# A feed-forward-heavy encoder block: another planning pass, another set of seven-product units, row factors moved to ScalarE

## The chip, the core and the metric

The kernel runs on one core of a Trainium2 chip. The metric is device time in microseconds for one execution; lower is better. The engines that matter are TensorE (PE, the matmuls), VectorE (DVE), ScalarE (ACT) and SyncE (SP), whose queue issues nearly all transfers. Each engine works through its own instructions in order, and they meet at semaphores.

## The reference

One layer of a streaming encoder with 256 rows of 2048 numbers in float32. It has four residual parts in a row and a last normalisation. The parts this case is about are the first and the last, two gated feed-forward nets with a hidden width of 5632:

```python
def swiglu(h, w_gate, w_up, w_down):
    return (jax.nn.silu(h @ w_gate) * (h @ w_up)) @ w_down

x = x + 0.5 * swiglu(rms_norm(x, ffn1_norm[l]), ffn1_w_gate[l], ffn1_w_up[l], ffn1_w_down[l])
h = rms_norm(x, mix_norm[l])
proj = h @ w_in[l]
...
x = x + jnp.concatenate([y_pool, y_gla], axis=-1) @ w_out[l]
x = x + mem_cross_attention(rms_norm(x, xattn_norm[l]), rms_norm(mem, mem_norm[l]),
                            xattn_w_q[l], xattn_w_kv[l], xattn_w_o[l])
x = x + 0.5 * swiglu(rms_norm(x, ffn2_norm[l]), ffn2_w_gate[l], ffn2_w_up[l], ffn2_w_down[l])
return rms_norm(x, final_norm)
```

`rms_norm` divides a row by its root mean square and multiplies by a gain. The row's divisor can be applied after a matmul, because it is one factor for the whole row; the kernel does that, and calls it the row factor, `Rcol`.

## The kernel before

**Numbers in two halves.** Every float32 operand is split into a high part, which ScalarE casts (`wh`, `xh`), and the rest, which VectorE subtracts (`wl`, `xl`). A product is then three matmuls: high by high, high by low, low by high (`products`, and the inner loop of `seven`).

**Units.** The work on weights is cut into units. A unit brings 1 MB of weights into a `raw` tile (128 partitions x 2048 numbers), splits it and multiplies it with the activations. There are four `raw` tiles and three `wh` and three `wl` tiles, so a split can be two units ahead of its matmuls. A `block_s` is eight units on one 1024-column block of the gate or up weights: 256 rows by 2 x 128 contraction rows by 1024 columns in each unit.

**Two kinds of unit.** A plain unit (`unit_p`) takes 8 products, so 24 matmuls of 512 columns. A unit of seven (`unit_s`, `seven`) uses a Strassen-Winograd scheme: 7 products, 21 matmuls. For it VectorE has to form four sums of quarter blocks in place, each reading or overwriting what the one before it used (`split_seven`: four additions `raw<-raw`), and two splits in place of one (`xh`, `xl` of 1536 numbers before the sums, `wh`, `wl` of 2048 after them). On the activation side the sums are formed once for a net (`part_sums`, `gate_sums`; they overwrite a part of `xs`, so a unit must have been used as a plain one before). `PAIRS` lists which of the eight units of a gate or up block are units of seven.

**PSUM.** There are four PSUM tiles, each of 2 x 512 numbers. A `block_s` needs all four: two for the products P1, P6, P7, P5 (`parts`), which `combine` empties as soon as the last unit of seven is done, and two (`ps`) in which P2, P3, P4 and all the plain products add up, and which are emptied at the block's end. A plain unit uses the second two only. The next block takes the tiles that were given back first. The transposes of the hidden values (`turn`) need two tiles for a while as well, and come a set number of units after their block.

**Evictions.** At a gate block's end VectorE adds `combine`'s sums to the products (`joined_to`, into a tile `sg`), and ScalarE applies `silu(Rcol * x)`. At an up block's end VectorE adds the sums in the same way and multiplies by the row factor and by the gate in two instructions (`ev_up`). Blocks come in the order gate, up, gate, up; an odd last block holds 512 columns of each (`wtwo`). The hidden columns are done in three parts of 4, 4 and 3 blocks of 512 (`FF_PARTS`), each followed by its down projection with its own pairs (`DOWN_PAIRS`), which the change doesn't touch.

**The planner.** The program first records every operation as a task with an engine, an estimated cost and what it depends on, then plans an order for each engine, and emits that order; the chip follows it. TensorE's matmuls keep the program's order except where one isn't ready. `latest` gives each task a latest start, backward from the end, without regard to what else its engine has to do. `schedule` then walks forward in time: an engine takes, of the tasks ready within 0.2 us (`WAIT`), the one with the smallest latest start. `ready` says when a task can begin: behind a task of another engine, at that task's end plus 0.034 us (`SYNC`) with its tail (0.085 us on VectorE); behind one of its own engine that only read what it overwrites, at once. All instructions appear in the profile under one line, L456, where the recorder issues them, so groups are told apart by their tiles.

Of the kernel before, what the change touches and what calls it, by code (L numbers as in the profile page):

```python
# [12 lines left out]
AF = mybir.ActivationFunctionType  # L13
ALU = mybir.AluOpType
# [190 lines left out]
class Plan:  # L205
# [104 lines left out]
    def ready(self, t, end):  # L310
        r = 0.0
        for p, data in t.preds.items():
            if p.engine is None:
                x = p.start
            elif p.engine == t.engine and not p.moved and (p.engine == "tensor" or not data):
                x = p.start + p.busy
            else:
                x = end[p.i] + self.SYNC
            r = max(r, x)
        return r  # L320

    def latest(self):
        for t in self.tasks:
            t.succs = []
        for t in self.tasks:
            for p in t.preds:
                p.succs.append(t)
        chain = [t for t in self.tasks if t.engine == "tensor"]
        behind = dict(zip(chain, chain[1:]))
        left = [len(t.preds) for t in self.tasks]  # L330
        for t in chain[1:]:
            left[t.i] += 1
        order = [t for t in self.tasks if not left[t.i]]
        for t in order:
            for s in (*t.succs, *([behind[t]] if t in behind else ())):
                left[s.i] -= 1
                if not left[s.i]:
                    order.append(s)
        assert len(order) == len(self.tasks)
        for t in reversed(order):  # L340
            late = -t.busy - t.tail
            for s in t.succs:
                if t.engine is None:
                    x = s.late
                elif t.moved:
                    x = s.late - 2.0 - t.moved / 338e3
                elif s.engine == t.engine and (t.engine == "tensor" or not s.preds[t]):
                    x = s.late - t.busy
                else:
                    x = s.late - t.busy - t.tail - self.SYNC  # L350
                late = min(late, x)
            if t in behind:
                late = min(late, behind[t].late - t.busy)
            t.late = late

    def schedule(self):
        self.share()
        self.latest()
        n = len(self.tasks)
        end, left = [0.0] * n, [len(t.preds) for t in self.tasks]  # L360
        free = {e: 0.0 for e in ("vector", "scalar", "tensor", "gpsimd", "sync")}
        waiting = {e: [] for e in free}
        tables, wire, out = {}, 0.0, []

        def release(t):
            todo = [t]
            while todo:
                t = todo.pop()
                for s in t.succs:
                    left[s.i] -= 1  # L370
                    if not left[s.i]:
                        s.start = self.ready(s, end)
                        if s.engine is None:
                            end[s.i] = s.start
                            out.append(s)
                            todo.append(s)
                        else:
                            waiting[s.engine].append(s)

        for t in self.tasks:  # L380
            if not t.preds:
                t.start = 0.0
                if t.engine is None:
                    out.append(t)
                    release(t)
                else:
                    waiting[t.engine].append(t)

        def pick(e):

            q, now = waiting[e], free[e]
            if e == "tensor":
                now = max(now, min(t.start for t in q))
                t = min((t for t in q if t.start <= now), key=lambda t: t.i)
                return now, t
            soon = max(now, min(t.start for t in q))
            u = min((t for t in q if t.start <= soon + self.WAIT), key=lambda t: t.late)
            if u.start > soon:
                fit = [t for t in q if t.start <= soon and soon + t.busy <= u.start]
                if fit:  # L400
                    u = min(fit, key=lambda t: t.late)
            return max(now, u.start), u

        while any(waiting.values()):
            at, t, _ = min(
                ((*pick(e), k) for k, e in enumerate(free) if waiting[e]),
                key=lambda x: (x[0], x[2]),
            )
            e = t.engine
            waiting[e].remove(t)  # L410
            t.start = at
            busy = t.busy * (2 if e == "tensor" and at < self.SLOW else 1)
            if t.table and tables.get(e) != t.table:
                tables[e] = t.table
                busy += 1.28
            free[e] = at + busy
            end[t.i] = at + busy + t.tail
            if t.moved:
                wire = max(wire, at + 2.0) + t.moved / 338e3
                end[t.i] = wire  # L420
            out.append(t)
            release(t)
        assert len(out) == n, (len(out), n)
        self.end = end
        out = [t for _, _, t in sorted((t.start, k, t) for k, t in enumerate(out))]
        return out

    WAIT = 0.2
    SLOW = 9.0

    def emit(self):
# [8 lines left out]
class Recorder:  # L440
# [3 lines left out]
    def __getattr__(self, name):  # L444
        def call(*args, **kw):
            plan, e = self.plan, self.engine
            views = [a for a in (*args, *kw.values()) if isinstance(a, View)]
            writes = [v for k, v in kw.items() if k in ("out", "accum_out") and isinstance(v, View)]
            if "out" not in kw and isinstance(args[0], View):
                writes.append(args[0])  # L450
            reads = [v for v in views if not any(v is w for w in writes)]

            def run():
                real = lambda a: a.resolve() if isinstance(a, View) else a
                f = getattr(getattr(plan.tc.nc, e), name)
                return f(*(real(a) for a in args), **{k: real(a) for k, a in kw.items()})  # L456

            t = plan.add(e, run, **cost(e, name, args, kw, writes, reads))
            t.f32 = e == "tensor" and name == "matmul" and args[1].dtype is F32
            t.what = (name, [v.buf.name for v in writes], [v.buf.name for v in reads])  # L460
            for v in reads:
                plan.touch(t, v, False)
            for v in writes:
                plan.touch(t, v, True)
            return t
        return call


def build(ctx, tc, I, out):
    nc = plan = Plan(tc)  # L470
    st = Stream()
# [69 lines left out]
    Rcol = ctl("Rcol", [P, 2])  # L541
# [3 lines left out]
    chain = ctl("chain", [P, 2, 8])  # L545
# [480 lines left out]

    FF_PARTS = ((0, 4), (4, 4), (8, 3))

    PAIRS = (0, 2, 4, 6)
    DOWN_PAIRS = {16: (2, 5), 12: (2, 4)}  # L1030
    OUT_PAIRS = (3, 5)

# [8 lines left out]
    def gate_sums(pairs):  # L1041

        for g in pairs:
            if not len(xe) % (len(PAIRS) + 1):
                xe.clear()
                xe["all"] = local([P, len(PAIRS), 2, 3, P], F32R, tag="xe", name=uid("xe"))
            xe[g] = xe["all"][:, PAIRS.index(g)]
            part_sums(xs, xe[g], g)

    def folded(c):  # L1050
        gate_sums([g for g in PAIRS[1:] if g // 2 == c])

    def ffn(wg, wu, wd, down, first=()):
        gate = {}
# [11 lines left out]
        def ev_gate(j, c, fresh):  # L1066

            if fresh and fresh == 1 + j:
                gate["new"] = hidden()
            g = gate["new"][j] if fresh else c  # L1070
            gate[j] = g
            for h in range(2):
                nc.scalar.activation(g[:, h, :], c[:, h, :], AF.Silu, scale=Rcol[:, h : h + 1])

        def ev_up(j, c):
            g = gate[j]
            for h in range(2):
                nc.vector.scalar_tensor_tensor(
                    out=g[:, h, :], in0=c[:, h, :], scalar=Rcol[:, h : h + 1], in1=g[:, h, :],
                    op0=ALU.mult, op1=ALU.mult,  # L1080
                )

        def turn(g, k):

# [8 lines left out]
        for lo, n in FF_PARTS:  # L1093
            for b in range(0, n - 1, 2):
                n0 = (lo + b) * NB
                pairs = first if lo == b == 0 else PAIRS
                if pairs:
# [306 lines left out]
    for b in range(2):  # L1404
        block_b(wblock(w_in, (4 + b) * NB), xs, ev_v(b))
        for i in range(2):
            h = 2 * b + i
# [229 lines left out]
            st.unit(wwide(wd, b * 2 * NB, k0 + nk - 2, 2)[0], end_unit(b))  # L1637
        st.op(second_half)

    st.op(lambda: gate_sums(PAIRS[:1]), 1)  # L1640
    ffn(I["ffn2_w_gate"][0], I["ffn2_w_up"][0], I["ffn2_w_down"][0], down_last, PAIRS[1:])
    st.op(close_scope)

# [64 lines left out]
```

## Time and profile before

| what | us |
|---|---|
| median of 3 runs | 2122.88 (2122.63 to 2125.29) |
| the profiled execution | 2122.68 |
| its span, first to last instruction | 2120.8 |
| granted TensorE clock, mean | 0.998 of full |
| HBM read and written | 417.58 MB and 16.78 MB |

The first net runs from the start to about 722 us, the mixer, attention and their projections to about 1397 us, the second net to the end. A profile's page lists busy time by engine, the span in 40 equal slices (a digit is the busy share in tenths), the chain of work that ended last, and the costliest groups of instructions. In a group's row stand the count, the busy time (overlaps counted once), the mean duration of one in ns, and the engine's idle time just before them with what ended it. A row of waits says which engine and tile waited for which, the total in us, how often, and the longest. A row of windows gives, for one stretch of time, its length and each engine's busy time with its number of instructions, then the granted clock, the DMA share and GB/s. A timeline row has start, duration, engine and instruction.

### The profile page before, as it was taken

The page shows a single profiled execution, that of the slowest core. Times are in us where ns is not written, and L with a number is a line of the kernel's source. Part 1 is how long each engine was busy: PE and PEld are TensorE (multiplying, and loading weights), DVE is VectorE, ACT ScalarE, POOL GpSimd, SP SyncE. Part 2 cuts the span into 40 slices and gives each one's busy share as a digit, 9 for nine tenths or more (in the row PEclk, how much of TensorE's full clock was granted, in tenths as well). Part 3 has the DMA queues.
Part 4 walks back from the last instruction along what each step waited for, and adds up shares of the span by engine and source line. Part 5 has one row for each costly group of instructions (what it writes and reads, how often), then busy time and mean ns, then how long its engine had stood idle before and what let it go on. Part 6 is the DMA issues. An engine that isn't in the chain of part 4 may idle for free.

```text
span 2120.8 us, 24464 instructions
## 1 busy us (share of the span) xinstructions
PE 2089.4 (99%) x9861; PEld 1732.5 (82%) x9861; DVE 1799.5 (85%) x1731; ACT 1102.5 (52%) x1002; POOL 15.8 (1%) x41
## 2 busy tenths in 40 slices
PE   9999999999999999999999999999999999999998
PEld 7878878788788888888888888887788877887886
DVE  7999889999899977688765545999998999988984
ACT  7555454554545645455654344556554455454543
POOL 0000000000000000000000000000000000000001
PEclk9999999999999999999999999999999999999999
DMA  7555756567565655457755555765567655675572
GB/s 280 197 195 203 257 199 212 188 234 245 182 220 207 240 181 181 157 179 258 239 182 174 164 174 159 238 199 199 179 218 258 214 186 184 229 254 202 185 273 98
DMA packets 143320, 435.94 MB, mean 206 GB/s; under 512 B 9828, under 2 KB 13000, under 8 KB 142824
## 3 DMA queue, kind: packets, MB, share of 16 engines
q1 hardware_dynamic: 143176, 434.38, 60.2%
q8 instruction: 77, 1.26, 0.2%
q14 instruction: 35, 0.29, 0.0%
q10 hardware_dynamic: 32, 0.01, 0.0%
HBM read 417.58 MB, written 16.78 MB: 205 GB/s over the span
## 4 chain that ended last, share of the span: by engine, by line
PE 54%; DVE 34%; issue 6%; ACT 3%; DMA 2%; SPq 0%; DVEq 0%; ACTq 0%
PE pt L456 27%; PE pa L456 15%; DVE wl L456 14%; DVE raw L456 8%; PE pb L456 6%; DVE xl L456 5%; DVE sg L456 5%; PE pe L456 3%; ACT wh L456 3%; DMA raw<-in_ffn_w_gate 1%; DVE ys L456 1%; DMA raw<-in_ffn_w_up 1%; DVE T L456 1%; DVE x L456 1%; PE pv L456 1%
## 5 line engine op out<-in xcount | busy, mean ns | idle before, releaser
L456 ACT CAST wh<-raw 128x2048 fp32r<-128x2048 f32 (+2 forms) x383 | 718.4, 1885 | 630.8 <-DVE raw L456 323.5
L456 DVE TENSOR_TENSOR wl<-raw,wh 128x2048 fp32r<-128x2048 f32 (+2 forms) x382 | 856.7, 2258 | 198.6 <-ACT wh L456 197.6
L456 PE MATMUL pt<-wh,xs 128*128 128x512 f32 x1820 | 590.4, 391 | 6.5 <-DVE sg L456 4.5
L456 PE MATMUL pt<-wh,ys 128*128 128x512 f32 x1392 | 441.3, 390 | 0.0
L456 PEld LDWEIGHTS pt<-wh,xs 128*128 128x128 f32 x1820 | 342.8, 188 | 78.3 <-issue 6.4
L456 PE MATMUL pt<-wl,xs 128*128 128x512 f32 x910 | 359.6, 395 | 7.4 <-DVE wl L456 7.2
L456 PE MATMUL pa<-xs,wh 128*128 128x512 f32 x912 | 320.1, 397 | 0.0
L456 DVE TENSOR_TENSOR raw<-raw 128x512 f32<-128x512 f32 x444 | 306.8, 691 | 13.4
L456 PEld LDWEIGHTS pt<-wh,ys 128*128 128x128 f32 x1392 | 261.2, 188 | 54.7 <-issue 0.2
L456 PE MATMUL pt<-wl,ys 128*128 128x512 f32 x696 | 271.2, 390 | 0.5 <-DVE wl L456 0.5
L456 PE MATMUL pa<-xs,wl 128*128 128x256 f32 x896 | 248.5, 280 | 0.0
L456 ACT CAST xh<-raw 128x1536 fp32r<-128x1536 f32 x111 | 164.5, 1482 | 153.6 <-PE pt L456 45.0
L456 PEld LDWEIGHTS pt<-wl,xs 128*128 128x128 f32 x910 | 171.4, 188 | 54.3 <-DVE wl L456 20.6
L456 PEld LDWEIGHTS pa<-xs,wh 128*128 128x128 f32 x912 | 170.8, 188 | 39.8 <-issue 0.7
L456 DVE TENSOR_TENSOR xl<-raw,xh 128x1536 fp32r<-128x1536 f32 x111 | 194.3, 1750 | 9.3 <-ACT xh L456 9.1
L456 PEld LDWEIGHTS pa<-xs,wl 128*128 128x128 f32 x896 | 169.1, 189 | 1.2
L456 PEld LDWEIGHTS pt<-wl,ys 128*128 128x128 f32 x696 | 130.7, 188 | 28.4 <-DVE wl L456 1.9
L456 DVE TENSOR_TENSOR sg<-pt,sg 128x1024 f32<-128x1024 f32 (+1 forms) x147 | 140.8, 966 | 9.9 <-ACT sg L456 7.0
L456 PE MATMUL pb<-wh,xs 128*128 128x512 f32 x384 | 121.9, 392 | 0.0
L456 PE MATMUL pt<-wh,xe 128*128 128x512 f32 x332 | 121.1, 393 | 0.0
L456 PE MATMUL pt<-xh,xs 128*128 128x512 f32 x332 | 119.6, 390 | 0.6 <-DVE sg L456 0.6
L456 PEld LDWEIGHTS pb<-wh,xs 128*128 128x128 f32 x384 | 72.1, 188 | 15.2 <-issue 0.3
(179 smaller groups left out, 1777.4 us busy)
## 6 DMA issues: line engine op xcount, KB each, us to landing
raw<-in_ffn_w_down SPq DMA_DIRECT2D x88, 1024.0 KB, 5.5
raw<-in_ffn_w_up SPq DMA_DIRECT2D x80, 1024.0 KB, 5.1
raw<-in_ffn_w_gate SPq DMA_DIRECT2D x77, 1024.0 KB, 5.1
raw<-in_w_in SPq DMA_DIRECT2D x32, 1024.0 KB, 5.2
raw<-in_xattn_w_kv SPq DMA_DIRECT2D x32, 1024.0 KB, 5.3
raw<-in_w_out SPq DMA_DIRECT2D x16, 1024.0 KB, 5.6
raw<-in_xattn_w_q SPq DMA_DIRECT2D x16, 1024.0 KB, 5.2
raw<-in_xattn_w_o SPq DMA_DIRECT2D x16, 1024.0 KB, 5.4
```

The costliest lines, as they stand in the source:

```text
L456: return f(*(real(a) for a in args), **{k: real(a) for k, a in kw.items()})
```

## The change

1. In the planner, an engine's own earlier tasks are no longer free to follow: any dependence, except between two TensorE tasks, costs the tail and `SYNC`.
2. VectorE's costs are taken 1% higher (`MARGIN`).
3. `schedule` alternates up to six forward walks (`forward`, the walk of before) with backward ones (`backward`), which place tasks from the end with one engine doing one thing at a time and so set new latest starts. The forward walk with the earliest end, by the model, is kept.
4. `PAIRS` becomes (1, 2, 4, 5). What is written in terms of `PAIRS` moves with it: the transposes of a pair of blocks come after six units of the next block and not seven, the second net's first sums after two units and not one.
5. The row factor of the up product goes into the gate: ScalarE multiplies the gate by `Rcol` once more after the silu, and `ev_up` is one product of 1024 columns.

```diff
-            elif p.engine == t.engine and not p.moved and (p.engine == "tensor" or not data):
+            elif p.engine == t.engine == "tensor":
                 x = p.start + p.busy
...
-                elif s.engine == t.engine and (t.engine == "tensor" or not s.preds[t]):
+                elif s.engine == t.engine == "tensor":
                     x = s.late - t.busy
...
     def schedule(self):
         self.share()
         self.latest()
+        best = None
+        for _ in range(self.ROUNDS):
+            out, end = self.forward()
+            if best is None or max(end) < best[0]:
+                best = max(end), out, end, [t.start for t in self.tasks]
+            self.backward()
+        _, out, self.end, starts = best
+        for t, at in zip(self.tasks, starts):
+            t.start = at
+        return out
+
+    ROUNDS = 6
+
+    def backward(self):
...
+        by = {t.i: t.start for t in self.tasks}
+
+        def bound(t):
+
+            x = 0.0
+            for s in t.succs:
+                if t.engine is None:
+                    x = min(x, s.late)
+                elif t.moved:
+                    x = min(x, s.late - self.SYNC - 2.0 - t.moved / 338e3 + t.busy)
+                elif s.engine == t.engine == "tensor":
+                    x = min(x, s.late)
+                else:
+                    x = min(x, s.late - t.tail - (self.SYNC if s.engine else 0.0))
+            return x
...
+        def pick(e):
+            q, now = waiting[e], free[e]
+            if e == "tensor":
+                for x, t in q:
+                    if t is chain[-1]:
+                        return min(now, x), (x, t)
+                return None
+            soon = min(now, max(x for x, _ in q))
+            x, t = max((c for c in q if c[0] >= soon - self.WAIT), key=lambda c: by[c[1].i])
+            return min(now, x), (x, t)
+
+        while any(waiting.values()):
...
+            t.late = at - t.busy
+            free[e] = t.late
+            release(t)
...
+    def forward(self):
...
     WAIT = 0.2
+    MARGIN = 1.01
...
             t = plan.add(e, run, **cost(e, name, args, kw, writes, reads))
+            if e == "vector":
+                t.busy *= plan.MARGIN
...
-    PAIRS = (0, 2, 4, 6)
+    PAIRS = (1, 2, 4, 5)
...
             for h in range(2):
                 nc.scalar.activation(g[:, h, :], c[:, h, :], AF.Silu, scale=Rcol[:, h : h + 1])
+            for h in range(2):
+                nc.scalar.activation(g[:, h, :], g[:, h, :], AF.Copy, scale=Rcol[:, h : h + 1])
 
         def ev_up(j, c):
-            g = gate[j]
-            for h in range(2):
-                nc.vector.scalar_tensor_tensor(
-                    out=g[:, h, :], in0=c[:, h, :], scalar=Rcol[:, h : h + 1], in1=g[:, h, :],
-                    op0=ALU.mult, op1=ALU.mult,
-                )
+            nc.vector.tensor_tensor(out=gate[j], in0=c, in1=gate[j], op=ALU.mult)
...
-    st.op(lambda: gate_sums(PAIRS[:1]), 1)
+    st.op(lambda: gate_sums(PAIRS[:1]), PAIRS[0] + 1)
     ffn(I["ffn2_w_gate"][0], I["ffn2_w_up"][0], I["ffn2_w_down"][0], down_last, PAIRS[1:])
```

More of the change, by code (lines that the diff above doesn't have):

```diff
@@ L358, in schedule, with release @@
         self.latest()
+        best = None
[10 more added lines that the diff above has]
+    def backward(self):
+        n = len(self.tasks)
+        for t in self.tasks:
+            t.late = None
+        left = [len(t.succs) for t in self.tasks]
+        free = {e: 0.0 for e in ("vector", "scalar", "tensor", "gpsimd", "sync")}
+        waiting = {e: [] for e in free}
+        wire = [0.0]
+        by = {t.i: t.start for t in self.tasks}
[11 more added lines that the diff above has]
+            return x
+        def release(t):
+            todo = [t]
+            while todo:
+                t = todo.pop()
+                for p in t.preds:
+                    left[p.i] -= 1
+                    if not left[p.i]:
+                        if p.engine is None:
+                            p.late = bound(p)
+                            todo.append(p)
+                        else:
+                            waiting[p.engine].append((bound(p), p))
+        for t in self.tasks:
+            if not t.succs:
+                if t.engine is None:
+                    t.late = 0.0
+                    release(t)
+                else:
+                    waiting[t.engine].append((-t.tail, t))
+        left_on = {e: sum(t.engine == e for t in self.tasks) for e in free}
+        chain = [t for t in self.tasks if t.engine == "tensor"]
+        def pick(e):
[9 more added lines that the diff above has]
+        while any(waiting.values()):
+            e, at, c = None, None, None
+            for k in free:
+                if waiting[k]:
+                    got = pick(k)
+                    if got and (at is None or got[0] > at):
+                        e, (at, c) = k, got
+            t = c[1]
+            waiting[e].remove(c)
+            if e == "tensor":
+                chain.pop()
+            t.late = at - t.busy
+            free[e] = t.late
+            release(t)
+        for t in self.tasks:
+            assert t.late is not None
@@ L423, in schedule @@
         assert len(out) == n, (len(out), n)
-        self.end = end
         out = [t for _, _, t in sorted((t.start, k, t) for k, t in enumerate(out))]
-        return out
+        return out, end
     WAIT = 0.2
+    MARGIN = 1.01
     SLOW = 9.0
```

## The prediction

> **What bounds the kernel now.** I read the page first, for who is busy where.
>
> ```profile
> span 2120.8 us, 24464 instructions
> PE 2089.4 (99%) x9861; PEld 1732.5 (82%) x9861; DVE 1799.5 (85%) x1731; ACT 1102.5 (52%) x1002; POOL 15.8 (1%) x41
> ...
> DVE  7999889999899977688765545999998999988984
> ...
> PE 54%; DVE 34%; issue 6%; ACT 3%; DMA 2%; SPq 0%; DVEq 0%; ACTq 0%
> ```
>
> TensorE is busy all the time, yet a third of the chain that ended last is VectorE. VectorE's nines lie in slices 2 to 14 and 27 to 38: the two feed-forward nets. So two engines run nearly level there. The windows cut by stage say how much TensorE loses. The gate and up stages are rows 1, 3, 4, 5 and 6; row 2 is a down projection.
>
> ```profile
> core 0: us, PE busy (x) PEld busy (x) DVE busy (x) ACT busy (x) POOL busy (x), PEclk, DMA share, GB/s
> 269.79:439.40 169.61, 167.54 (x738) 135.91 (x736) 162.41 (x140) 90.89 (x63) 0.00 (x0) 1.00 0.58 204
> 439.40:525.99 86.59, 86.53 (x389) 71.38 (x388) 80.27 (x70) 41.03 (x27) 0.00 (x0) 1.00 0.67 231
> 525.99:653.72 127.73, 125.73 (x558) 102.31 (x556) 120.43 (x100) 66.67 (x44) 0.00 (x0) 1.00 0.60 208
> 1397.28:1572.60 175.32, 170.93 (x757) 137.89 (x756) 171.56 (x174) 103.56 (x91) 0.00 (x0) 1.00 0.58 197
> 1659.39:1829.01 169.62, 167.51 (x737) 135.93 (x736) 162.32 (x140) 89.45 (x62) 0.00 (x0) 1.00 0.59 203
> 1915.61:2044.75 129.14, 126.91 (x558) 103.67 (x556) 120.56 (x100) 65.05 (x43) 0.00 (x0) 0.99 0.60 206
> ...
> 454.66 64.04 PE pt L456 x282
> ...
> 660.62 1.03 PE L456 MATMUL ph<-ident,sg 128*128 128x128 f32 x8
> ```
>
> The last two rows give TensorE's pace where nothing stops it: 64.04 / 282 = 0.227 us for a matmul of 512 columns, and about 0.11 us for a 128-column transpose (eight in 1.03 us, with the last one's tail). A unit of seven products has 21 such matmuls, 4.77 us; a plain one 24, 5.45 us. Row 1 is four blocks of four units each, 4 x (84 + 96) = 720 matmuls, 163.5 us, and 16 transposes, 1.7 us: 4.4 us of 169.6 are lost. In the same way the others lose 3.4 (540 matmuls), 7.6 (723, and 32 transposes), 4.4 and 4.8 us, and the down stage 0.4. That is **24.6 us in five stages**, the most that they can give back. VectorE is 93 to 98% busy in them.
>
> Who ends the waits, and what VectorE's steps cost:
>
> ```profile
> PE pt L456 <- DVE wl L456: 8.6, 19, 1.5
> PE pt L456 <- DVE sg L456: 5.0, 5, 1.1
> ...
> PE pt L456 <- ACT xs L456: 2.0, 1, 2.0
> ...
> 403.27 1.75 DVE L456 TENSOR_TENSOR xl<-raw,xh 128x1536 fp32r<-128x1536 f32 x1
> 405.05 2.87 DVE L456 TENSOR_TENSOR raw<-raw 128x512 f32<-128x512 f32 x4
> 407.84 4.49 DVE L456 TENSOR_TENSOR wl<-raw,wh 128x2048 fp32r<-128x2048 f32 x2
> 412.24 1.75 DVE L456 TENSOR_TENSOR xl<-raw,xh 128x1536 fp32r<-128x1536 f32 x1
> ```
>
> From 403.27 to 412.24 VectorE does one unit of seven and one plain: 8.97 us. The two wl take 4.40 to the next start, 2.20 each, so a plain unit costs VectorE **2.2 us** and one of seven **6.8 us**, against 5.45 and 4.77 us of TensorE. A block's units take 36 us of 41; sums, evictions and transposed splits bring VectorE level with TensorE or past it. Three buffers of split weights let it be two units ahead of TensorE, no more.
>
> **The change, part by part.** *Row factors on ScalarE.*
>
> ```profile
> L456 DVE TENSOR_TENSOR sg<-pt,sg 128x1024 f32<-128x1024 f32 x77 | 92.7, 1220 | 2.1
> L456 DVE SCALAR_TENSOR_TENSOR sg<-sg,Rcol,sg 128x512 f32<-128x512 f32 x40 | 27.8, 745 | 0.1
> L456 ACT ACTIVATE sg<-sg,Rcol 128x512 f32<-128x512 f32 x40 | 25.9, 713 | 18.1 <-DVE sg L456 18.1
> L456 ACT COPY sg<-pt 128x512 f32<-128x512 f32 x35 | 20.5, 586 | 85.9 <-PE pt L456 80.2 <-DVE wl L456 5.7
> ...
> 654.97 1.34 ACT L456 ACTIVATE sg<-sg,Rcol 128x512 f32<-128x512 f32 x2
> 657.66 1.40 DVE L456 SCALAR_TENSOR_TENSOR sg<-sg,Rcol 128x512 f32<-128x512 f32 x2
> ```
>
> ev_up drops two scalar_tensor_tensor and adds one 1024-wide product. By busy time, which counts overlapped tails once, that is 2 x 27.8/40 = 1.39 against 92.7/77 = 1.20 us: 0.19 us saved; by mean durations, 2 x 745 - 1220 = 270 ns. The nearest row of the product reads PSUM and the new one reads SBUF alone; I take no gain for that. There are 11 column blocks in each net, so 22 x 0.19 = **4.1 us** less VectorE work (5.9 by durations). Some falls where VectorE has room, so I count 3.3.
> ScalarE gets 44 scaled copies of 0.59 to 0.71 us, 26 to 31 us. It is 52% busy, and in a full pair of blocks the scaled gate is read a whole block later, some 40 us, so the copies hide behind its idle time. Without that cover they stand before the wh casts, 1.2 to 1.4 us a block. The tight place is the odd block at a part's end, where gate and up share one block: silu at 654.97, product at 657.66 to 659.06, transposes at 660.62. Two copies more take up most of the 1.6 us left there; I price it at 0, at worst 1.2 us twice.
>
> *PAIRS.* Two things move. First, the sums' evacuation (combine) now comes after the sixth unit, with two plain units behind it, and the next block starts plain. What it does today at a boundary, in the chain of waits and TensorE's timeline:
>
> ```profile
> 305.63 1.92 ACT wh L456
> ...
> 307.57 2.29 DVE wl L456
> 309.87 0.61 DVE sg L456
> ...
> 310.50 1.24 DVE sg L456
> ...
> 311.76 0.70 DVE sg L456
> ...
> 312.60 0.47 PE L456 MATMUL pt<-wh,xs 128*128 128x512 f32 x1 [1.12 <-DVE sg L456]
> ...
> 1957.50:1959.20 1.70, 0.62 (x3) 0.18 (x2) 1.56 (x3) 0.33 (x1) 0.00 (x0) 1.00 0.85 188
> 1959.20:1962.50 3.30, 3.27 (x8) 2.63 (x9) 3.30 (x3) 2.00 (x4) 0.00 (x0) 0.53 0.54 221
> ```
>
> VectorE waited for the wh cast, did a 2.29 us wl, and only then combine, while the next block's first products wanted the same PSUM tiles. Today they have one plain unit, 5.45 us, to come free; after the change two, 10.9 us, and the new block first takes the tiles that were freed earliest. So the five sg waits, 5.0 us, should go. With each goes about 0.2 us of restart (the 1.12 us wait stands for a start-to-start of 1.51 us instead of 0.23). At 1957 two of them lie together and the granted clock falls to 0.53 for 3.3 us: another 1.6 us. In all some 7.5 us.
> The Trainium skill (TensorE: Matmul & The Clock Gate, "Why this matters for your kernels") lets the clock fall only behind idle gaps of about 3 us. By that rule the 1.6 us isn't the gap's and stays. The trace disagrees: the fall follows waits of 0.6 and 1.1 us.
> The ACT xs wait, 2.0 us, is the second net's late S3 part, made for the new block's first unit of seven; that unit now comes second, 5.45 us later. It should go too. Sum of waits that lose their cause: 7.5 + 2.2 = 9.7 us.
> But VectorE works on without a pause behind these places, so part of what TensorE gains there it meets again as a wl wait. I take half, **4.9 us** (ends 0 and 9.7).
> Second, two units of seven now stand side by side twice a block. That is a demand, priced as a rival below.
>
> *The planner.* It counts 0.119 us for every dependent VectorE step; before, a step that only overwrites what the last one read was free. The rows above decide who is right.
>
> ```profile
> L456 DVE TENSOR_TENSOR raw<-raw 128x512 f32<-128x512 f32 x444 | 306.8, 691 | 13.4
> ```
>
> Four raw steps in a row take 2.87 us where 4 x 0.691 = 2.76: each starts 0.03 us after its predecessor's end. Independent wl overlap: 4.49 for two of 2.29, 0.09 before the end. So a dependent step costs 0.12 us more, as the new plan says; the old one left out three per unit of seven, 444/4 = 111 units x 0.36 = 40 us of VectorE work, and took the engine for freer than it is.
> The Trainium skill (VectorE: DVE Perf Modes, "Rules for kernel authors") says of chained steps that the drain "happens regardless" and only the number of operations counts. By that rule the new term would be an error and the order would get no better. The trace disagrees, by the 0.12 us.
> A truer plan makes no work vanish; it can move what isn't due out of the way of wl. Up to six forward and backward passes are tried and the best end in the model is kept. Of the 8.6 us of wl waits I count 1.5 (ends -3 and 8.6).
>
> **Sum.** 3.3 + 4.9 + 1.5 = 9.7 us. The profiled execution took 2122.68 us, its span 2120.8; the median of the three runs is 2122.88, so both stand for one state. 2122.7 - 9.7 = **2113 us**.
>
> **Rivals.** One more window belongs here, from the boundary shown above to the last late wl of the stage:
>
> ```profile
> 309.87:454.22 144.35, 142.28 (x634) 115.08 (x633) 142.26 (x125) 79.94 (x57) 0.00 (x0) 1.00 0.57 197
> ```
>
> *VectorE's work is the bound (2120).* In this window VectorE is busy for 142.26 of 144.35 us, so only its work counts there, and a wait removed comes back as another. Against it: row 1 has 169.61 - 162.41 = 7.2 us of VectorE idle, 5 us of it ahead of 309.87, which a smoother order could use. It would leave 3.3 us or less: 2119.4 to 2123. That the plan's order comes out almost as before ends here too.
> *The plan recovers most (2102).* If order and buffers are the fault and not work, 20 of the 24.6 us come back; the idle 7.2 us of row 1, more than its 4.4 us of loss, allow it. 2098 to 2106.
> *Side by side (2130).* From a block's first unit to its second pair, VectorE owes evictions of 4 x 1.2 = 4.8 us, four units of seven (27.2) and one plain (2.2): 34.2 us, against 2 x 5.45 + 3 x 4.77 = 25.2 us of TensorE. It must be 9.0 us ahead. Today's worst stretch, from the end of the seventh unit to the third of the next block, is combine 2.5 (the three sg rows above), evictions 2.4 + 2.8, units 6.8 + 2.2 + 6.8: 23.5 us against 15.7, so 7.8 us ahead. If the lead that the buffers allow lies between, each boundary of the ten pairs loses up to 1.2 us, and no gain of the waits remains: 2122.7 - 3.3 + 12 = 2131, or 2127 if two thirds of it come. It decides when wl waits come in front of a block's sixth unit. Against it: two units, about 10 us, is more than 9.0.
>
> **How the numbers follow.** Forecast 0.50 (2107 to 2118), plan recovers most 0.23, work bound 0.18, side by side 0.09. About 0.2% (4.2 us) is what a measurement of this kernel can tell from no change, so faster ends at 2118.6 and slower begins at 2127.1. Faster: 0.50 + 0.23 + 0.03 of the work bound's edge = 0.76; same 0.16; slower 0.08, with 0.01 of the side-by-side case inside no change. The range, 2100 to 2122, leaves out the lower edge of the recovery case (0.05), the upper one of the work bound (0.03) and the side-by-side case (0.09).
>
> **What would show it.** Right: no sg wait before a pt matmul and no clock of 0.53 at a boundary; raw, wl and xl groups as before in number; the SCALAR_TENSOR_TENSOR group on sg gone, 22 products of about 1.2 us in its place and 44 ScalarE copies near 0.6 us; the five stages together 6 to 12 us shorter. Wrong: wl waits that grow by what the sg waits lose (work bound), or that stand before the sixth unit of a block (side by side); transposes of the odd block waiting for sg (the copies' price); a loss in the mixer or the attention between 722 and 1397 us, which I expect unchanged within 2 us.

## The result and the profile after

The changed kernel takes 2107.48 us (median of 4 runs, 2106.91 to 2110.4) against 2122.76 before (four runs beside them): ratio 0.9929, 95% interval 0.9912 to 0.9947, 15.3 us less. Forecast were 2113 us and a range of 2100 to 2122. The profiled execution is the longest of the four, 2110.4 us with a span of 2108.6, so the profile shows 12.2 of the 15.3 us.

The page after, the lines that answer to those of before:

```profile
span 2108.6 us, 24534 instructions
PE 2083.8 (99%) x9861; PEld 1734.4 (82%) x9861; DVE 1790.3 (85%) x1709; ACT 1133.0 (54%) x1046; POOL 15.8 (1%) x41
...
PE 64%; DVE 21%; ACT 6%; issue 5%; DMA 4%; SPq 0%; ACTq 0%; DVEq 0%
```

TensorE's work is the same (x9861), and its share of the chain that ended last rose from 54 to 64%: VectorE holds it up less. The same five stages, cut anew at their own borders (columns as before):

```profile
266.49:435.40 168.91, 167.28 (x738) 135.97 (x736) 165.29 (x136) 96.01 (x69) 0.00 (x0) 1.00 0.59 210
...
521.52:647.53 126.01, 125.29 (x557) 102.66 (x556) 122.37 (x100) 69.78 (x49) 0.00 (x0) 1.00 0.59 213
1389.18:1566.22 177.04, 171.63 (x756) 139.44 (x755) 170.49 (x168) 109.07 (x97) 0.00 (x0) 0.99 0.57 195
1652.34:1820.03 167.69, 166.80 (x738) 136.16 (x736) 163.79 (x135) 95.53 (x69) 0.00 (x0) 1.00 0.59 206
1906.12:2032.36 126.24, 125.64 (x557) 102.43 (x556) 123.27 (x100) 68.35 (x47) 0.00 (x0) 1.00 0.61 217
```

Together 765.9 us against 771.4: 5.5 us of the 12.2. Four are shorter; the second net's first stage, is 1.7 us longer. Most of the rest lies where the forecast didn't look, shown here before and then after for the first net's first stage, its last down projection, and the mixer and attention:

```profile
6.58:183.33 176.75, 174.03 (x775) 142.36 (x774) 164.45 (x176) 108.63 (x119) 0.00 (x0) 1.00 0.64 225
653.72:722.26 68.54, 67.10 (x303) 53.84 (x302) 65.82 (x71) 36.58 (x41) 0.00 (x0) 1.00 0.62 222
722.26:1397.28 675.02, 675.02 (x3593) 578.53 (x3592) 471.82 (x519) 340.92 (x388) 5.28 (x12) 1.00 0.59 193
```

```profile
6.83:180.38 173.55, 173.17 (x776) 142.09 (x774) 163.23 (x169) 112.97 (x125) 0.00 (x0) 1.00 0.65 229
647.53:714.24 66.71, 66.02 (x302) 54.12 (x300) 63.53 (x68) 37.60 (x42) 0.00 (x0) 1.00 0.62 218
714.24:1389.18 674.94, 674.94 (x3594) 578.96 (x3592) 472.82 (x520) 341.56 (x388) 5.26 (x12) 1.00 0.59 193
```

3.2 and 1.8 us shorter, and the middle of the kernel unchanged. The other three down projections are 0.5 to 0.7 us shorter each. TensorE's waits after:

```profile
PE pt L548 <- DVE wl L548: 7.6, 14, 1.4
...
PE pt L548 <- ACT xs L548: 0.8, 1, 0.8
PE pt L548 <- DVE x L548: 0.6, 2, 0.3
```

The five sg waits (5.0 us) are gone, and the wl waits went down with them, 8.6 to 7.6 us. That was not a matter of course: the forecast let half of what is gained at the boundary come back there.

### The profile page after: what moved, and what is told of

The parts are those of the page before. It is cut to its first block, busy times and chain, and to the rows that moved or that the text cites. A ratio compares the mean times of both kernels' runs of the same rounds, so it can differ in the third digit from the quotient of the medians.

```text
span 2108.6 us, 24534 instructions
## 1 busy us (share of the span) xinstructions
PE 2083.8 (99%) x9861; PEld 1734.4 (82%) x9861; DVE 1790.3 (85%) x1709; ACT 1133.0 (54%) x1046; POOL 15.8 (1%) x41
## 4 chain that ended last, share of the span: by engine, by line
PE 64%; DVE 21%; ACT 6%; issue 5%; DMA 4%; SPq 0%; ACTq 0%; DVEq 0%
PE pt L548 37%; PE pa L548 15%; DVE wl L548 8%; PE pb L548 6%; DVE raw L548 5%; DVE xl L548 3%; ACT wh L548 3%; PE pe L548 3%; DMA raw<-in_ffn_w_gate 2%; DVE sg L548 2%; DMA raw<-in_ffn_w_up 2%; ACT sg L548 2%; DVE x L548 1%; PE ph L548 1%; PE pv L548 1%
## 5 line engine op out<-in xcount | busy, mean ns | idle before, releaser
L548 DVE TENSOR_TENSOR raw<-raw 128x512 f32<-128x512 f32 x444 | 306.7, 691 | 12.2
L548 PEld LDWEIGHTS pb<-wh,xs 128*128 128x128 f32 x384 | 72.1, 188 | 15.2 <-issue 0.2
```

## The experiments

Three theories stood against each other. **Boundary:** the gain comes from where evictions fall around a block's end. **Work:** VectorE's work is the bound, and 4 us less of it is what counts. **Plan:** the order was at fault. Each part was tried alone and each was taken out. The table gives medians and ratios against the runs of before that were made beside them (2122.2 to 2123.0 us).

| kernel | planner | PAIRS | row factor on | us | ratio, 95% interval |
|---|---|---|---|---|---|
| planner only | new | old | VectorE | 2118.76 | 0.9982 (0.9973 to 0.9990) |
| PAIRS only | old | new | VectorE | 2118.14 | 0.9978 (0.9969 to 0.9987) |
| rows only | old | old | ScalarE | 2125.97 | 1.0019 (1.0010 to 1.0028) |
| without rows | new | new | VectorE | 2107.05 | 0.9928 (0.9916 to 0.9941) |
| without PAIRS | new | old | ScalarE | 2114.31 | 0.9955 (0.9942 to 0.9967) |
| without planner | old | new | ScalarE | 2118.05 | 0.9980 (0.9971 to 0.9989) |

**Planner only.** The changed kernel with the old PAIRS and the old `ev_up`.

```diff
-    PAIRS = (1, 2, 4, 5)
+    PAIRS = (0, 2, 4, 6)
...
```

> Before with the planner's part alone (dependent steps counted, 1% margin, six passes); PAIRS (0, 2, 4, 6) and the row factor on VectorE as before. Boundary theory (the gain is the place of the evictions): 2120 to 2122 us, the sg waits before pt still about 5 us. Work theory (VectorE's work is the bound): no change, 2122 to 2123. Plan theory (the order was at fault): 2112 or less, the sg waits gone though PAIRS are the old ones.

3.4 us by medians, inside no theory's range. No sg wait before pt is left, though the PAIRS are the old ones; TensorE's waits name wl 11.1 us instead. So the order alone can take those waits away, and they come back elsewhere. They come back in long pieces, and the granted clock (the third number from the end of a window row) falls with them, by TensorE's waits, its timeline and the windows:

```profile
PE pt L548 <- DVE wl L548: 11.1, 14, 2.4
...
PE pt L548 <- ACT xs L548: 3.1, 1, 3.1
...
1779.62 0.50 PE L548 MATMUL pt<-wl,xs 128*128 128x512 f32 x1 [2.44 <-DVE wl L548]
...
387.77:391.18 3.41, 2.92 (x7) 2.23 (x8) 3.41 (x4) 2.28 (x2) 0.00 (x0) 0.50 0.55 137
1439.08:1442.49 3.41, 3.41 (x10) 2.73 (x10) 3.41 (x3) 0.00 (x0) 0.00 (x0) 0.50 0.54 217
1521.00:1527.83 6.83, 5.81 (x18) 4.84 (x19) 5.52 (x5) 3.42 (x3) 0.00 (x0) 0.50 0.55 166
1780.41:1783.82 3.41, 3.41 (x13) 2.92 (x12) 3.41 (x3) 1.18 (x2) 0.00 (x0) 0.50 0.89 294
```

Three of the four stretches come with a wl wait of 2.4 us right behind the transposes of `turn`, seven units into the next block; the other comes with the wait for ACT xs. The clock is at half for 17.1 us, and TensorE is busy for 15.6 of them, work that takes half as long at the full clock: an estimate of some 8 us lost, where the kernel before loses 1.6 in its one such stretch. The profiled execution is not a chance one: all eleven show a mean clock of 0.994 to 0.996, and the twenty-seven of before that were made beside them 0.998 on average. So, by this estimate, most of what the planner could give alone goes into these stretches.

**PAIRS only.** The edit above the other way round, in the kernel before, with the second net's first sums after `PAIRS[0] + 1` units.

> Before with PAIRS (1, 2, 4, 5) alone, old plan, row factor on VectorE. Boundary theory: 2112 to 2116 us, no sg wait before pt. Work theory: 2121 to 2123, wl waits grow by what the sg waits lose. Plan theory: with the old plan the side-by-side units cost, 2122 to 2128.

4.1 us, between the ranges of boundary and work. TensorE's waits of this kernel:

```profile
PE pt L456 <- DVE wl L456: 11.5, 27, 1.0
...
PE pt L456 <- DVE sg L456: 1.0, 1, 1.0
```

Four of the five sg waits went (5.0 to 1.0 us), and wl waits rose from 8.6 to 11.5: most of it came back, as the work theory has it. The 2.0 us wait for ACT xs and the stretch of 0.53 clock are gone too.

**Rows only.** `ev_gate` and `ev_up` as in the change, all else before.

> Before with the row factor on ScalarE alone. Work theory: 4.1 us of VectorE work less, 2118 to 2119 us. Boundary theory: the waits have another cause than work, 2120 to 2122. Plan theory: 2121 to 2123.

Slower by 0.19%, beyond every theory's number. The sg waits before pt are still there (5.1 us) and the wl waits are 9.8.

**Without rows.** The changed kernel with the two `scalar_tensor_tensor` back in `ev_up` and no scaled copy.

> The changed kernel with the row factor back on VectorE (planner and PAIRS kept). Work theory: it gives back 4 us or more of the 15, 2111 to 2115 us. Boundary and plan theory: 1 to 3 us, 2108 to 2110.

2107.05 us, as fast as the whole change (2107.48) and below every range: the row factors are worth nothing here, though VectorE is busy 4.0 us longer without them (1794.3 against 1790.3).

**Without PAIRS**, the changed kernel with (0, 2, 4, 6), and **without planner**, the kernel before with PAIRS and row factors:

> The changed kernel with PAIRS back at (0, 2, 4, 6) (planner and row factors kept). Boundary theory: it gives back 6 to 9 us, 2114 to 2117, and sg waits before pt come back. Plan theory: 2108 to 2110 us. Work theory: 2107 to 2109.

> Before with PAIRS and row factors of the change but the old planner. Boundary theory: 2108 to 2112 us. Plan theory: most of the gain is gone, 2118 to 2122. Work theory: 2117 to 2119.

Without PAIRS 2114.31 us, inside the boundary theory's 2114 to 2117, but not for its reason: only 1.0 us of waits for sg before pt is back, while the wl waits are 10.6 us (7.6 in the change), the wait for ACT xs is 3.1 (0.8), and two stretches of half clock of 3.4 us each follow wl waits behind the transposes. Without planner 2118.05 us, inside the plan theory's 2118 to 2122 and the work theory's 2117 to 2119. Both give back more than the part is worth alone: PAIRS 4.1 alone and 6.8 in the changed kernel, the planner 3.4 alone and 11.1 on top of PAIRS (2118.14 to 2107.05, timed side by side). **The gain is neither part but the two together**: the planner takes waits away, and the PAIRS keep it from the long waits at the transposes and the half clock behind them. That the clock makes up most of this difference, some 8 us in the kernel with the planner alone and none inside the one with both, is an estimate from the traces; no run held the clock up under the old PAIRS.

Which part of the planner is it? **One walk** (no backward pass), **old price** (dependent steps free as before in the forward walk and in `latest`, no margin, six passes kept), and **no margin** (one walk and VectorE's costs as they were, so that the counting is all that is left):

```diff
-    ROUNDS = 6
+    ROUNDS = 1
...
-    MARGIN = 1.01
+    MARGIN = 1.0
```

> The changed kernel with one forward walk (ROUNDS = 1, no backward pass; dependent steps and margin still counted). If the backward passes matter: 2110 to 2114 us. If the counting of dependent steps is what the planner gives: 2106 to 2109.

> The changed kernel with the old price of dependent steps in the forward walk and no margin, six passes kept. If the counting matters: 2110 to 2114 us. If the backward passes are what the planner gives: 2106 to 2109.

> The changed kernel with one forward walk and VectorE's margin at 1.0: only the counting of dependent steps is left of the planner's change. If the counting alone carries the gain: 2102 to 2105 us as with the margin. If the margin carries it: 2112 to 2118.

One walk: 2102.84 us, ratio 0.9906 (0.9893 to 0.9920), faster than the whole change; no run of it (2102.44 to 2104.28) comes near the change's 2106.91 to 2110.4. Old price: 2118.62 us, 0.9982 (0.9973 to 0.9991), beyond both ranges and the gain of the planner gone with the six passes in place. No margin: 2101.86 us, 0.9902 (0.9888 to 0.9916), as with it. So, with the new PAIRS, **the counting of dependent steps is the planner's whole gain**: against before, 21.1 us where it is all that is left of the planner, beside 4.5 us without any of it. The backward passes take some 5 us back, by kernels that were not timed side by side; neither expectation for one walk had that. Some 1.5 us of it, an estimate, is a stretch of half clock that the profiled execution of the change has and those with one walk have not (the last section).

What an order planned with the counting does differently is seen at one place of the first net's second part, 53 us into the stage, in VectorE's and TensorE's timelines. Without planner:

```profile
311.67 2.28 DVE L456 TENSOR_TENSOR wl<-raw,wh 128x2048 fp32r<-128x2048 f32 x1
313.87 1.22 DVE L456 TENSOR_TENSOR sg<-pt,sg 128x1024 f32<-128x1024 f32 x1
315.00 2.86 DVE L456 TENSOR_TENSOR raw<-raw 128x512 f32<-128x512 f32 x4
318.29 4.49 DVE L456 TENSOR_TENSOR wl<-raw,wh 128x2048 fp32r<-128x2048 f32 x2 [0.43 <-ACT wh L456]
...
322.84 0.50 PE L456 MATMUL pt<-wl,xs 128*128 128x512 f32 x1 [0.75 <-DVE wl L456]
```

With one walk:

```profile
308.69 2.35 DVE L548 TENSOR_TENSOR sg<-pt,sg 128x1024 f32<-128x1024 f32 x2
310.95 2.28 DVE L548 TENSOR_TENSOR wl<-raw,wh 128x2048 fp32r<-128x2048 f32 x1
313.15 2.87 DVE L548 TENSOR_TENSOR raw<-raw 128x512 f32<-128x512 f32 x4
315.93 2.28 DVE L548 TENSOR_TENSOR wl<-raw,wh 128x2048 fp32r<-128x2048 f32 x1
318.71 2.29 DVE L548 TENSOR_TENSOR wl<-raw,wh 128x2048 fp32r<-128x2048 f32 x1 [0.49 <-ACT wh L548]
...
321.05 0.50 PE L548 MATMUL pt<-wl,xs 128*128 128x512 f32 x1
```

In the first order one eviction stands behind the first wl, and both remaining wl wait behind the four sums and ScalarE's cast; the second of them ends at 322.8 and TensorE waits 0.75 us. In the second both evictions come early, one wl stands directly behind the sums, where nothing holds it, and the other is done in time. What the stage gains, by the windows of the kernel without margin, beside rows 1, 3 and 4 of the first windows after:

```profile
267.04:433.54 166.50, 166.36 (x738) 136.42 (x736) 163.51 (x136) 96.03 (x69) 0.00 (x0) 1.00 0.59 209
1385.56:1560.42 174.86, 170.55 (x757) 137.82 (x755) 170.48 (x168) 108.58 (x97) 0.00 (x0) 1.00 0.58 198
1646.54:1812.83 166.29, 166.16 (x737) 136.38 (x736) 163.32 (x136) 95.83 (x69) 0.00 (x0) 1.00 0.59 208
...
PE pt L548 <- DVE wl L548: 3.0, 6, 1.2
```

The two stages of four blocks are at 166.3 to 166.5 us where 165.2 is TensorE's own work (163.5 + 1.7): a loss of 1.1 to 1.3 us where it was 4.4 before. VectorE is idle in the first for 3.0 us, against 7.2 before and 3.6 in the change. Its work hardly changed; it idles less.

**Rows without copies.** Is it ScalarE's 44 copies that eat the saving? The kernel before with the short `ev_up` and no copies, which leaves the row factor of the up product out:

```diff
-            g = gate[j]
-            for h in range(2):
-                nc.vector.scalar_tensor_tensor(
...
+            nc.vector.tensor_tensor(out=gate[j], in0=c, in1=gate[j], op=ALU.mult)
```

> Before with the up product as one 1024-wide VectorE product and no scaled copy anywhere: the row factor of the up half is left out, so this shows the VectorE saving without ScalarE's 44 copies. If the copies ate the saving: 2118 to 2120 us. If 4 us less VectorE work is worth nothing under the old order, whatever ScalarE does: 2122 to 2127.

2125.01 us, ratio 1.0010 (1.0001 to 1.0020): inside the second range. There is no gain, though VectorE is busy 2.9 us less (1796.6 against 1799.5) and ScalarE has nothing more to do. The difference to 1.0019 with the copies, some 0.1%, isn't clear of the noise: the two intervals overlap. TensorE's waits for sg before pt are 6.6 us here, against 5.0, so the order planned from the shorter work may have given away what it left free; at which step was not traced.

**Another place for the units of seven.** PAIRS (0, 1, 5, 6) has two neighbouring pairs as the change has, but a block begins with a unit of seven and one plain unit follows `combine`, as before. The transposes move back to after seven units with it, and the second net's first sums to after one.

```diff
-    PAIRS = (1, 2, 4, 5)
+    PAIRS = (0, 1, 5, 6)
```

> The changed kernel with PAIRS (0, 1, 5, 6): two neighbouring pairs of units of seven as in the change, but the block starts with a unit of seven and one plain unit follows the sums, as before. Boundary theory (the plain units around the block's end give the gain): 2113 to 2116 us like the kernel with the old PAIRS. Neighbour theory (two units side by side give each other independent VectorE steps): 2106 to 2110, with some 80 exposed dependent steps fewer than the old PAIRS.

2123.80 us, ratio 1.0005 (0.9996 to 1.0014): the whole gain lost, some 9 us more than with the old PAIRS under the same planner and beyond both ranges. Its waits:

```profile
PE pt L548 <- DVE sg L548: 8.5, 12, 2.3
PE pt L548 <- DVE ys L548: 6.4, 4, 2.0
...
PE pt L548 <- ACT xs L548: 4.5, 1, 4.5
PE pt L548 <- DVE wl L548: 1.6, 3, 0.8
```

sg is the tile of the evictions at a block's end; ys takes the transposes, whose PSUM tiles ScalarE and VectorE read out. The granted clock is at half in three stretches of 3.4 us besides. The neighbour theory falls: neighbours do share steps (VectorE starts that follow a predecessor's end by 0 to 0.06 us, counted in the whole trace: 609 before, 549 with PAIRS alone, 506 here), but the kernel with the fewest is among the slowest. The boundary theory had the direction, not the size. Which of the things that moved costs the most, the first unit, the plain ones at the end, the transposes or the sums, wasn't separated.

**A lighter start of the second net.** Its first stage is the one that got longer. One walk, and only units 4 and 5 of its first block as units of seven:

```diff
-    ROUNDS = 6
+    ROUNDS = 1
...
-    st.op(lambda: gate_sums(PAIRS[:1]), PAIRS[0] + 1)
+    st.op(lambda: gate_sums(PAIRS[:2]), PAIRS[1] + 1)
...
```

> One forward walk, and the second net's first block with two units of seven, (4, 5), in place of three; their sums for the other two are formed after its third unit. That block's stage loses the most (9.7 us). If VectorE's work there is the bound, 7 us less of it against 0.7 us more TensorE work: 2098 to 2101 us. If the stage's loss is order alone: 2102 to 2105.

2102.36 us, ratio 0.9904 (0.9890 to 0.9918): inside the range for order alone, and no faster than the other two kernels with one walk. VectorE is busy for 1784.0 us where the kernel without margin has 1789.8, and again no gain that the runs tell apart.

## Why the prediction was right, and where it wasn't

Direction and range held; the sum of 9.7 us was made of three terms, and the measured 15.3 are not their sum. That the time still lies inside the forecast's own 2107 to 2118 is in part luck: one term was worth nothing and another several times its size, and the two errors go opposite ways.

- **Row factors, 3.3 us: this step failed.** The sizes were right: the new product takes 23.9/20 = 1.20 us as forecast from the PSUM row, the copies are 44 more ScalarE instructions of 714 ns (31 us), and the odd block's transposes didn't wait for them. What failed is the step from "less VectorE work" (4.0 us less busy, by the kernel without rows beside the change) to "I count 3.3", that is, work read as time. Three kernels say no: without rows 2107.05 against 2107.48, rows only +0.19%, rows without copies +0.10%.

```profile
L548 DVE TENSOR_TENSOR sg<-sg,sg 128x1024 f32<-128x1024 f32 x20 | 23.9, 1222 | 0.3
L548 ACT ACTIVATE sg<-sg,Rcol 128x512 f32<-128x512 f32 x84 | 54.7, 714 | 10.2 <-DVE sg L548 9.4 <-DVE Rcol L548 0.8
```

- **PAIRS, 4.9 us between 0 and 9.7: right in size and mechanism under the old planner.** Alone it gave 4.1 us; the sg waits went and most came back as wl waits. It missed what PAIRS do under the new planner, where they are worth 6.8 us with rows on ScalarE (2114.31 to 2107.48) and 11.7 with rows on VectorE (2118.76 to 2107.05): there the old PAIRS bring waits of up to 2.4 us behind the transposes, and two and four stretches of half clock. The wait for ACT xs went from 2.0 to 0.8 us and not to nothing, and the new stretch of half clock at 1405 takes back what the one at 1959 cost.
- **The planner, 1.5 us between -3 and 8.6: too small.** Alone 3.4 us, on top of PAIRS 11.1, beyond the upper end. The reading behind it was right, a dependent step costs 0.12 us and three per unit weren't counted; "a truer plan makes no work vanish" was right too, but it was priced as if it could only push a few wl around. The passes were taken as harmless and cost some 5 us: one walk is faster.
- **The rivals.** "VectorE's work is the bound" is spoken against by the kernels that took work away and gained nothing. "The plan recovers most", 2098 to 2106 us, is where the kernels with one walk are; the change itself came halfway, since its backward passes cost some 5 us. "Side by side" didn't happen with (1, 2, 4, 5): PAIRS alone made the kernel faster. With (0, 1, 5, 6) a price came in another form, waits for evictions and for the tiles of the transposes.
- **What would show it.** The sg waits and the 0.53 clock at the boundary are gone, the groups are as listed, the middle of the kernel is unchanged. The five stages are 5.5 us shorter, just under the 6 to 12 given, since the second net's first one lost 1.7.

The Trainium skill (VectorE: DVE Perf Modes, "Rules for kernel authors") says to minimise the number of chained operations, not the semaphores between them. The runs speak against planning by that rule here: with the new PAIRS, the price of 0.12 us a dependent step in the plan is worth 16 us (2118.05 us without any of the new planner, 2101.86 with that price alone).

Open: why six passes end worse than one walk. The kept walk is the best by the model's end; that the model and the chip part by more than the passes differ is likely, and wasn't tried. Open too is whether PAIRS need the counting, or just any order in which the two wl come in time, and which step of the plan leaves wl late behind the transposes under the old PAIRS.

## What to carry to other kernels

- Where two engines run level and one has 95% busy time, take work away from it in an experiment before pricing that work as time; here 4 us less gave 0, and a new order (PAIRS and plan) of nearly the same work gave 21.
- A plan by estimated costs is worth as much as its smallest repeated term: a step that overwrites what the engine's last step read isn't free, and with 0.12 us times 333 steps uncounted the planner chose orders for an engine that didn't exist.
- Test the parts of a change in pairs. Planner and PAIRS gave 3.4 and 4.1 us alone and 15.2 together, and one part of the planner, the passes, was a loss. Look at the granted clock in each of them before reading a difference as the worth of a part.

## What the runs showed of the hardware that was not expected

TensorE's granted clock again fell to half behind short waits, now at another place. In the changed kernel the second net's first stage has waits of 0.36 and 1.40 us within 3 us, and then, by TensorE's timeline and the windows:

```profile
1403.06 0.47 PE L548 MATMUL pt<-wh,xs 128*128 128x512 f32 x1 [0.36 <-DVE xs L548]
...
1405.16 0.79 PE L548 MATMUL pt<-wl,xs 128*128 128x512 f32 x1 [1.40 <-DVE wl L548]
...
1405.10:1408.40 3.30, 3.24 (x8) 2.56 (x9) 3.27 (x4) 0.00 (x0) 0.00 (x0) 0.51 0.62 179
```

For 3.3 us the clock is 0.51: matmuls start 0.43 us apart and not 0.23, which makes, as an estimate, some 1.5 us of the 1.7 that this stage lost. The length of the waits doesn't settle it. Before, 0.58 and 1.11 us together brought the fall, and the single 2.0 us for ACT xs none; here, 60 us later, two waits of nearly the same length brought none, by the timeline and the window behind them:

```profile
1462.94 0.50 PE L548 MATMUL pt<-wh,xs 128*128 128x512 f32 x1 [0.37 <-ACT wh L548]
1464.66 0.50 PE L548 MATMUL pt<-wl,xs 128*128 128x512 f32 x1 [1.22 <-DVE wl L548]
...
1464.60:1467.00 2.40, 2.34 (x10) 1.97 (x11) 1.68 (x2) 2.40 (x4) 0.00 (x0) 1.00 0.53 94
```

So waits of 1 to 2 us can cost 1.6 us on top, and needn't. What tells the two places apart is seen when the trace is cut into the right pieces. The fourteen traces of this case, by their clock records, have thirteen falls before the kernel's end; each begins a whole multiple of 3.413 us after the clock was first granted in full, and lasts one such piece, or once two. In pieces of this grid, the first row ends where the fall begins, and the other two hold the place 60 us later:

```profile
1401.76:1405.17 3.41, 1.65 (x8) 0.74 (x6) 3.41 (x5) 1.64 (x1) 0.00 (x0) 1.00 0.00 0
...
1459.79:1463.20 3.41, 3.04 (x14) 2.16 (x12) 3.31 (x5) 2.27 (x3) 0.00 (x0) 1.00 0.01 6
1463.20:1466.61 3.41, 2.19 (x10) 1.61 (x10) 2.69 (x2) 3.41 (x5) 0.00 (x0) 1.00 0.30 40
```

In the first pair both waits lie in one piece, and TensorE is busy for 0.48 of it; in the second they lie in two, 0.89 and 0.64. Over all traces, up to 2090 us, the piece ahead of a fall is busy for 0.00 to 0.51 of its time, and every other one for 0.52 or more, but for one: in the kernel before, the piece with the 2.0 us wait for ACT xs has 0.45 and no fall behind it (the same wait lies in a piece of 0.41 in the two kernels with rows under the old plan and PAIRS, and brings one there). So it counts how much idle time falls into one piece, and a shift of a microsecond can decide it. This is read from the traces; no run shifted a wait to try it, and the one exception is unexplained.
